# Merging the bursts of a woven recurrence, moving its loads, and giving Pool some subtractions at the start

## The chip, the cores and the metric

The kernel runs on one core of a Trainium2 chip. The metric is the time of one execution on the device in microseconds, the median of three runs. The engines are named as in the profile: PE multiplies matrices, DVE (vector), ACT (scalar) and POOL (GpSimd) do the rest, and SP issues every DMA, all on one queue.

## The reference

One decoder layer for 2048 tokens of width 1024. The normalised input is projected to 4 mLSTM heads (q, k, v, gates o and z) and 2 SSD groups (z, x, B, C, dt, a causal convolution of 4 taps). Each head and each group runs a recurrence over chunks of 128 tokens; both results are gated, normalised, put beside each other, projected back and added to the input.

```python
h = rms_norm(x, norm_w[l])
proj = h @ w_in[l]
...
hm = mlstm_chunkwise(q, k, v, log_i, log_f)            # per head: C <- s_old C + s_loc k^T v; h = (S v + q C) / denom
hm = hm * lax.rsqrt(jnp.mean(hm * hm, axis=-1, keepdims=True) + EPS)
hm = hm * mlstm_norm_w[l] * sigmoid(o_pre) * silu(z_m)
...
y = ssd_chunked(xs, dt, A, Bm, Cm)                     # per group: H <- exp(a) H + B^T (decay x dt); y = (C B^T * decay) x dt + C H
y = (y + d_skip * xs) * silu(z_s)
y = y * lax.rsqrt(mean over the group of y * y + EPS) * ssd_norm_w[l]
x = x + concatenate([hm, y]) @ w_out[l]
return rms_norm(x, final_norm_w)
```

## The kernel before, in words

**The products.** The input projection and the output projection are done as 68 jobs of 7 products each, after Strassen: 2 halves of the tokens (s = 0, 1) with 26 column pairs each (4 pairs for each head h0 to h3, 5 for each group g0, g1, in the phases h0, g0, h1, h2, h3, g1), then 16 jobs of the output projection. A product is 12 matmuls of 128x512 (L270): each operand is split into a high and a low part (names ending in h and l), and high times high, high times low and low times high are summed. The right operands of a product are named R11, R21, R22 and T1 to T4 (token side; they stay in L390 DMA R22h<-ws0R_186 128x2048
L390 DMA R22l<-ws0R_186 128x2048
L346 DMA gd_1_111<-oa 128x1024
L346 DMA gd_1_111<-ob 128x1024
L390 DMA T4h<-ws0T_187 128x2048
L390 DMA T4l<-ws0T_187 128x2048
L788 DMA gin<-gd_1_111 128x6x128
L795 DMA E<-arow_150 128x1024
L803 DMA ea<-arow_150 64x4x128 x2UF for a stage and are loaded anew, "refilled", L390, when the stage changes), the left ones L11, L12, L22 and S1 to S4 (weight side; formed anew for every job: ACT copies the high part, L191, DVE subtracts for the low part, L192). After a product its result pj is taken out by ACT copies (L276, L283, L289, into oa, ob, ca, cbt) and DVE sums.

**The recurrences.** When a phase is done, its recurrence is run by a generator, rec_head or rec_group, while PE works on the jobs of the next phase: `step`, called once for each product, moves a clock on by one tick and calls `wv.to()`, and the class Weave then runs as many pieces of the generator (up to the next `yield`) as keep it in proportion to the phase (28 steps where four jobs follow, 35 where five, 42 in the output projection). What a piece puts on PE stands between two products; it is called a burst here. In `rec_head`, chunk n has: load (hin L676, nmi L678), scores (PE L694, L696; ACT w L690 from nmi; DVE st L698), memory (PE L714, L716, L718: the numerator and the state), then ACT sums squares (sj L731) and copies (mx L732), POOL scales (L733 to L735, mx), gate (loads and forms g, L742), and turn (PE transposes mx, L751; DVE multiplies by the gate, L752; a DMA stores it into mix, L753). In `rec_group`, chunk n has: load (gin L788), decay (DMA E L795, DVE L798, ACT exp L800; ea L803, L805), tokens (PE L813, L814, L817; DVE xw, xdt, cbm), then DVE E times cbm (L829), states (PE L845), update (PE L857), outs (PE L872, with 16 matmuls), then DVE and POOL form the gated squares q (L878 to L883), norm (PE L889; DVE r L891; POOL L892 and dg L894), and spread (PE L901; DVE L902; the store L903). A `later(k, ...)` puts a piece k ticks on: gate 1, turn 4, norm 3 and spread 5 ticks after the burst of their chunk.

**The rest.** The first tokens are normalised, turned and split by `start_h` while the first job already runs. From the phase after h1 on, a background generator does the other half's tokens (`next_h`, s = 0) or scales the output weights (`next_w`, s = 1: loads of wg, we L532, ACT scaling L533, splits L396 and L398, stores L537). The order of PE is that of the program. The instructions of the other engines and the DMAs on SP are put in order by the compiler's scheduler; buffers of a tag come from a ring of fixed size, so that a load waits for the last reader of its ring's slot.

Of the kernel before, what the change touches and what calls it, by code (L numbers as in the profile page):

```python
# [69 lines left out]
def hybrid_layer(ctx, tc, x, norm_w, w_in, b_igate, b_fgate, conv_w, conv_b, dt_bias,  # L70
# [32 lines left out]
    def r2(nm, n=512):  # L103
        return mk([P, n], "r2", 7, nm)

    def r1(nm, n=NV):
        return mk([P, 272], "r1", 6, nm)[:, 0:n]

    def r5(nm, n=P):
        return mk([P, n], "r5", 9, nm)  # L110
# [77 lines left out]
    def split(ops, o, src):  # L188
# [3 lines left out]
        nc.vector.tensor_sub(lo, v, hi.bitcast(F32))  # L192
# [156 lines left out]
    def out_pair(L, R, j, c):  # L349
# [18 lines left out]
        for i, t in enumerate((a, b)):  # L368
# [8 lines left out]
            nc.scalar.activation(mk([P, DM], "r2", 7, "fj", BF16), t, AF.Square, accum_out=sq)  # L377
# [23 lines left out]
    def tok_norm(r0, nwb, t):  # L401
# [3 lines left out]
        jk = mk([P, DM], "r2", 7, "jk", BF16)  # L405
# [17 lines left out]
    def start_h():  # L423
# [14 lines left out]
        def put(o, c, src):  # L438
# [3 lines left out]
            nc.vector.tensor_sub(lo, v, hi.bitcast(F32))  # L442
# [77 lines left out]
    def next_w():  # L520

        for j in range(2):
            for k in range(4):
# [4 lines left out]
                for a in range(2):  # L528
                    r = j * 8 + a * 4 + k
                    for b in range(2):  # L530
                        u = q[a, b]
                        nc.sync.dma_start(u, w_out[r * P:(r + 1) * P, b * TB:(b + 1) * TB])  # L532
                        nc.scalar.activation(u, u, AF.Copy, scale=nwo[:, r:r + 1])  # L533
                yield
# [133 lines left out]
    def rec_head(s, h):  # L668
# [3 lines left out]
        def load(n):  # L672
# [4 lines left out]
            nmi = r2("nmi", 2 * P).rearrange("p (a l) -> p a l", a=2)  # L677
# [29 lines left out]
        def memory(n):  # L707
# [11 lines left out]
            if C is None:  # L719
                C = S["C"] = mk([P, NV + 14], "C", 1, "C")[:, 0:NV]  # L720
# [10 lines left out]
            nc.scalar.activation(mk([P, DV], "r5", 9, "sj", BF16), nps[:, 0:DV], AF.Square, accum_out=sq)  # L731
# [23 lines left out]
        load(0)  # L755
        S["C"] = None
        if s:
            C = S["C"] = mk([P, NV + 14], "C", 1, "C")[:, 0:NV]
            nc.sync.dma_start(C, cd[h])
# [5 lines left out]
        for n in range(len(seq)):  # L765
            if n + 1 < len(seq):
                scores(n + 1)
# [3 lines left out]
            later(1, lambda n=n: gate(n))  # L771
            later(4, lambda n=n: turn(n))
            if n + 3 < len(seq):
                load(n + 3)
            yield

    def rec_group(s, g):
# [128 lines left out]
        decay(0)  # L906
        S["H"] = None
# [7 lines left out]
        for n in range(len(seq)):  # L915
            states(n)
            yield
            update(n)
# [3 lines left out]
            later(3, lambda n=n: norm(n))  # L922
            later(5, lambda n=n: spread(n))
# [6 lines left out]
            yield  # L930

# [3 lines left out]
    NREC = {"h": 10, "g": 25}  # L935

    class Weave:
# [3 lines left out]
        def set(self, g, n, total):  # L941
            self.finish()
            self.g, self.n, self.done, self.i, self.total = g, n, 1, 0, total
# [90 lines left out]
    for n, jb in enumerate(jobs):  # L1034
# [35 lines left out]
        if more:  # L1070
            next(jobs[n + 1]["gen"])
            step(n + 1, "R21")
        next(g)
# [4 lines left out]
        if "s" in jb and (n + 1 == len(jobs) or jobs[n + 1].get("ph") != jb["ph"]):  # L1078
            nxt = [k for k in jobs[n + 1:] if k.get("ph") == jobs[n + 1].get("ph") and k["stage"] == jobs[n + 1]["stage"]]
            wv.set(rec(jb["s"], jb["ph"]), NREC[jb["ph"][0]], 7 * len(nxt) if "s" in jobs[n + 1] else 42)  # L1080
# [35 lines left out]
```

## Time and profile before

| | |
|---|---|
| median of 3 runs | 1832.38 us (1822.41 to 1832.39) |
| profiled execution, its own time | 1829.99 us |
| its span, first to last instruction | 1828.2 us |
| mean granted TensorE clock | 0.966 |
| busy: PE / DVE / ACT / POOL | 1679.5 (92%) / 1308.7 (72%) / 880.6 (48%) / 450.2 us (25%) |
| DMA | 405.32 MB, mean 222 GB/s |

The span leaves out 1.8 us of the execution's own time. PE's busy time is that of its matmuls as the trace shows them; where the granted clock is below 1.00 the same matmul takes longer. Idle time of PE is split in the view of waits by what came last before the matmul that waited.

### The profile page before, as it was taken

The numbers are of one execution on the slowest core, as the hardware profiler recorded it, in microseconds if no ns is written. First come the engines' busy times: TensorE is split into PE (matmuls) and PEld (weight loads), VectorE is DVE, ScalarE is ACT, GpSimd is POOL, SyncE is SP. The second block draws the span as 40 slices with busy tenths as digits, with TensorE's granted clock in tenths as the row PEclk, the third lists the DMA queues.
The fourth block names the chain that finished last, engine by engine and source line by source line (L and its number), as shares of the span: only waits on it lengthen the run. The fifth ranks groups of instructions, "written<-read, shape, count | busy, mean of one in ns | idle before, by whom it ended". The sixth has DMA issues, their size and how long they took to land.

```text
span 1828.2 us, 25057 instructions
## 1 busy us (share of the span) xinstructions
PE 1679.5 (92%) x8072; PEld 1357.2 (74%) x8072; DVE 1308.7 (72%) x2417; ACT 880.6 (48%) x1880; POOL 450.2 (25%) x629
## 2 busy tenths in 40 slices
PE   4999999999899798989899999898988889997997
PEld 4688887778788685767788777777776667776885
DVE  7677968877567693888675895655678578864775
ACT  5344644456566663434564444655565433332443
POOL 2000413332122131223121331202211144532222
PEclk9999999999999899999999999999999989998999
DMA  5245666668787689655575658888877976678543
GB/s 153 93 156 174 185 212 203 207 212 256 224 258 231 181 274 379 206 182 179 161 203 185 196 181 272 290 278 263 258 260 250 384 260 212 205 265 315 189 158 115
DMA packets 358323, 405.32 MB, mean 222 GB/s; under 512 B 30224, under 2 KB 284432, under 8 KB 352816
## 3 DMA queue, kind: packets, MB, share of 16 engines
q1 hardware_dynamic: 358192, 403.72, 68.1%
q8 instruction: 64, 1.05, 0.2%
q14 instruction: 67, 0.55, 0.1%
HBM read 251.40 MB, written 152.24 MB: 221 GB/s over the span
## 4 chain that ended last, share of the span: by engine, by line
PE 25%; DMA 15%; DVE 7%; issue 3%; ACT 2%; SPq 1%; POOL 1%; DVEq 0%; POOLq 0%; ACTq 0%
PE pj L270 21%; DMA E<-arow 1%; DMA we<-in_w_out 1%; DVE E L798 1%; DMA nmi<-mrow 1%; DMA mx<-mix 1%; DMA gin<-gd 1%; DMA ws1R<-hqh 1%; DMA T4l<-ws1T 1%; DMA ws0T<-hql 1%; DMA ws0R<-hqh 1%; DMA ws0T<-hqh 1%; DMA xr<-in_x 1%; DMA ws1T<-hqh 1%; PE rc L872 1%
## 5 line engine op out<-in xcount | busy, mean ns | idle before, releaser
L733 POOL TENSOR_SCALAR sq<-dn,sq 128x1 f32<-128x1 f32 x64 | 46.1, 720 | 624.9 <-ACT sj L731 477.8
L270 PE MATMUL pj<-R22h,S4h 128*128 128x512 f32 x272 | 119.7, 440 | 38.1 <-ACT ob L289 24.6
L270 PE MATMUL pj<-T2h,S2h 128*128 128x512 f32 x272 | 113.4, 417 | 11.6 <-ACT ca L276 9.3
L270 PE MATMUL pj<-T1l,S1h 128*128 128x512 f32 x272 | 107.3, 395 | 7.6 <-DMA T1l<-ws1T 7.2
L270 PE MATMUL pj<-R22l,S4h 128*128 128x512 f32 x272 | 113.1, 416 | 0.0
L270 PE MATMUL pj<-T4h,L22h 128*128 128x512 f32 x272 | 111.5, 410 | 1.4 <-DMA T4h<-ws1T 1.4
L270 PE MATMUL pj<-R11h,L11h 128*128 128x512 f32 x272 | 112.7, 414 | 0.0
L270 PE MATMUL pj<-R22h,S4l 128*128 128x512 f32 x272 | 112.7, 414 | 0.0
L270 PE MATMUL pj<-T2l,S2h 128*128 128x512 f32 x272 | 109.0, 401 | 4.0 <-DMA T2l<-hsT 3.3
L270 PE MATMUL pj<-T1h,S1h 128*128 128x512 f32 x272 | 111.0, 408 | 1.4 <-ACT cbt L283 1.4
L270 PE MATMUL pj<-R21h,L12h 128*128 128x512 f32 x272 | 110.1, 405 | 0.0
L270 PE MATMUL pj<-T3h,S3h 128*128 128x512 f32 x272 | 109.3, 402 | 0.0
L270 PE MATMUL pj<-T2h,S2l 128*128 128x512 f32 x272 | 108.6, 399 | 0.0
L270 PE MATMUL pj<-T1h,S1l 128*128 128x512 f32 x272 | 107.2, 394 | 1.3 <-DVE S1l L192 1.3
L270 PE MATMUL pj<-T4l,L22h 128*128 128x512 f32 x272 | 106.6, 392 | 1.9 <-DMA T4l<-ws1T 1.9
L270 PE MATMUL pj<-T4h,L22l 128*128 128x512 f32 x272 | 106.7, 392 | 0.0
L270 PE MATMUL pj<-R11h,L11l 128*128 128x512 f32 x272 | 106.6, 392 | 0.0
L270 PE MATMUL pj<-R11l,L11h 128*128 128x512 f32 x272 | 106.5, 391 | 0.0
L270 PE MATMUL pj<-T3h,S3l 128*128 128x512 f32 x272 | 106.3, 391 | 0.0
L270 PE MATMUL pj<-R21l,L12h 128*128 128x512 f32 x272 | 106.3, 391 | 0.0
L270 PE MATMUL pj<-R21h,L12l 128*128 128x512 f32 x272 | 106.3, 391 | 0.0
L270 PE MATMUL pj<-T3l,S3h 128*128 128x512 f32 x272 | 106.3, 391 | 0.0
(330 smaller groups left out, 4697.4 us busy)
## 6 DMA issues: line engine op xcount, KB each, us to landing
wa<-in_w_in SPq DMA_DIRECT2D x52, 512.0 KB, 6.2
s<-sum SPq DMA_DIRECT2D x52, 512.0 KB, 5.3
hd<-ob SPq DMA_DIRECT2D x32, 512.0 KB, 3.8
E<-arow SPq DMA_DIRECT2D x32, 512.0 KB, 5.2
hin<-hd SPq DMA_DIRECT2D x64, 256.0 KB, 4.7
mx<-mix SPq DMA_DIRECT2D x32, 512.0 KB, 4.9
wb<-in_w_in SPq DMA_DIRECT2D x26, 512.0 KB, 4.2
sum<-ls SPq DMA_DIRECT2D x26, 512.0 KB, 4.6
```

What stands on the lines that cost most here:

```text
L270: nc.tensor.matmul(ps, lhsT=l[:, k, :], rhs=r[:, k, :], start=start and k + n == 0, stop=k == 3 and n == 2, skip_group_check=True)
L733: nc.gpsimd.tensor_scalar(sq, dn, DV * EPS, sq, op0=ALU.mult, op1=ALU.add)
L798: nc.vector.tensor_scalar(E[:, r, :], E[:, r, :], G["cum"][:, c, k:k + 1], 0.0, op0=ALU.subtract, op1=ALU.min)
L872: nc.tensor.matmul(yps[o:o + HD, (r // 2) * P:(r // 2 + 1) * P], lhsT=xdt[:, r * HD:(r + 1) * HD], rhs=E[:, r, :], start=True, stop=True, ...
```

## The change

In `rec_head` turn(n-1) now stands at the head of the burst with scores(n+1) and memory(n), and gate(n) in the same burst; the deferred calls are gone. In `rec_group` norm(n-1) stands ahead of states(n), and spread(n-1) ahead of update(n) and outs(n). The generators have more pieces (12 and 29), and Weave begins with two of them counted as done. The recurrence of a phase is created, and its first load issued, before the last two products of the phase's last job (`pre`). The scaling of output weights is put three yields behind their loads. Rings change (r2 7 to 6, r1 6 to 8 with nmi moved there, r5 9 to 8, C shares a tag with H). In the first tokens the low parts of T1 to T4 (16 subtractions), and of the left operands as long as the clock stands at 0 (6 subtractions: L11, L12 and S2, S3 of job 0, L11 of job 1, S1 of job 0), go from DVE to POOL. The ring sizes in calls are cut from the diff below.

```diff
@@ -101,13 +101,13 @@
         return mk([P, 1024], "t", 1, nm)
 
     def r2(nm, n=512):
-        return mk([P, n], "r2", 7, nm)
+        return mk([P, n], "r2", 6, nm)
 
     def r1(nm, n=NV):
-        return mk([P, 272], "r1", 6, nm)[:, 0:n]
+        return mk([P, 272], "r1", 8, nm)[:, 0:n]
 
     def r5(nm, n=P):
-        return mk([P, n], "r5", 9, nm)
+        return mk([P, n], "r5", 8, nm)
 
     ident = cst.tile([P, P], F32, name="ident")
     make_identity(nc, ident)
...
@@ -189,7 +189,7 @@
         hi, lo = (mk([P, 4, P], "lr", 10, o + k, F32R) for k in "hl")
         v = src.rearrange("p (k c) -> p k c", k=4)
         nc.scalar.copy(hi, v)
-        nc.vector.tensor_sub(lo, v, hi.bitcast(F32))
+        (nc.vector if clock[0] else nc.gpsimd).tensor_sub(lo, v, hi.bitcast(F32))
         ops[o] = (hi, lo)
 
     def left_sums(ops, a, b, save=None):
...
@@ -439,7 +439,7 @@
             hi, lo = (t[:, :, c * P:(c + 1) * P] for t in R[o])
             v = src.rearrange("p (k c) -> p k c", k=4)
             nc.scalar.copy(hi, v)
-            nc.vector.tensor_sub(lo, v, hi.bitcast(F32))
+            (nc.gpsimd if o[0] == "T" else nc.vector).tensor_sub(lo, v, hi.bitcast(F32))
 
         for c in range(NCH):
             tok_norm(None, nwb, xs[c])
...
@@ -530,8 +530,12 @@
                     for b in range(2):
                         u = q[a, b]
                         nc.sync.dma_start(u, w_out[r * P:(r + 1) * P, b * TB:(b + 1) * TB])
-                        nc.scalar.activation(u, u, AF.Copy, scale=nwo[:, r:r + 1])
-                yield
+                for _ in range(3):
+                    yield
+                for a in range(2):
+                    r = j * 8 + a * 4 + k
+                    for b in range(2):
+                        nc.scalar.activation(q[a, b], q[a, b], AF.Copy, scale=nwo[:, r:r + 1])
 
                 def dst(o, i, v):
                     nc.sync.dma_start(wsd[j][o][:, i, k, :], v)
...
@@ -674,7 +678,7 @@
             o = (b % 2) * TB + c * P
             t = r2("hin").rearrange("p (a l) -> p a l", a=4)
             nc.sync.dma_start(t, hd[s][h][:, 0:4, o:o + P])
-            nmi = r2("nmi", 2 * P).rearrange("p (a l) -> p a l", a=2)
+            nmi = r1("nmi", 2 * P).rearrange("p (a l) -> p a l", a=2)
             nc.sync.dma_start(nmi, mrowd[b][:, h, c * P:(c + 1) * P].partition_broadcast(P))
             L["in", n] = (t, nmi)
 
...
@@ -717,7 +721,7 @@
             cps = rc_tile()
             nc.tensor.matmul(cps[:, 0:NV], lhsT=kw, rhs=vt, start=True, stop=True)
             if C is None:
-                C = S["C"] = mk([P, NV + 14], "C", 1, "C")[:, 0:NV]
+                C = S["C"] = mk([P, GW], "H", 1, "C")[:, 0:NV]
                 nc.vector.tensor_copy(C, cps[:, 0:NV])
             else:
                 nc.vector.scalar_tensor_tensor(C, C, nmi[:, 1, P - 1:P], cps[:, 0:NV],
...
@@ -728,7 +732,7 @@
                                            op0=ALU.mult, op1=ALU.max)
             mx = r1("mx")[:, 0:DV]
             sq = mk([P, 1], "sq", 3, "sq")
-            nc.scalar.activation(mk([P, DV], "r5", 9, "sj", BF16), nps[:, 0:DV], AF.Square, accum_out=sq)
+            nc.scalar.activation(mk([P, DV], "r5", 8, "sj", BF16), nps[:, 0:DV], AF.Square, accum_out=sq)
             nc.scalar.copy(mx, nps[:, 0:DV])
             nc.gpsimd.tensor_scalar(sq, dn, DV * EPS, sq, op0=ALU.mult, op1=ALU.add)
             nc.gpsimd.tensor_tensor(sq, sq, mhalf, op=ALU.pow)
...
@@ -753,9 +757,10 @@
             nc.sync.dma_start(mixd[0][b * NCH + c][:, 2 * h:2 * h + 2, :], g)
 
         load(0)
+        yield
         S["C"] = None
         if s:
-            C = S["C"] = mk([P, NV + 14], "C", 1, "C")[:, 0:NV]
+            C = S["C"] = mk([P, GW], "H", 1, "C")[:, 0:NV]
             nc.sync.dma_start(C, cd[h])
         yield
         scores(0)
...
@@ -763,16 +768,19 @@
         load(2)
         yield
         for n in range(len(seq)):
+            if n:
+                turn(n - 1)
             if n + 1 < len(seq):
                 scores(n + 1)
             memory(n)
             if s == 0 and n + 1 == len(seq):
                 nc.sync.dma_start(cd[h], S["C"])
-            later(1, lambda n=n: gate(n))
-            later(4, lambda n=n: turn(n))
             if n + 3 < len(seq):
                 load(n + 3)
+            gate(n)
             yield
+        turn(len(seq) - 1)
+        yield
 
     def rec_group(s, g):
         seq = [(2 * s + i, c) for i in range(2) for c in range(NCH)]
...
@@ -904,6 +912,7 @@
 
         load(0)
         decay(0)
+        yield
         S["H"] = None
         if s:
             H = S["H"] = mk([P, GW], "H", 1, "H")
...
@@ -913,14 +922,16 @@
         load(1)
         yield
         for n in range(len(seq)):
+            if n:
+                norm(n - 1)
             states(n)
             yield
+            if n:
+                spread(n - 1)
             update(n)
             if s == 0 and n + 1 == len(seq):
                 nc.sync.dma_start(hdd[g], S["H"])
             outs(n)
-            later(3, lambda n=n: norm(n))
-            later(5, lambda n=n: spread(n))
             if n + 1 < len(seq):
                 decay(n + 1)
                 yield
...
@@ -928,11 +939,16 @@
                 if n + 2 < len(seq):
                     load(n + 2)
             yield
+        yield
+        norm(len(seq) - 1)
+        yield
+        spread(len(seq) - 1)
+        yield
 
     def rec(s, ph):
         return rec_head(s, int(ph[1])) if ph[0] == "h" else rec_group(s, int(ph[1]))
 
-    NREC = {"h": 10, "g": 25}
+    NREC = {"h": 12, "g": 29}
 
     class Weave:
         def __init__(self):
...
@@ -940,7 +956,7 @@
 
         def set(self, g, n, total):
             self.finish()
-            self.g, self.n, self.done, self.i, self.total = g, n, 1, 0, total
+            self.g, self.n, self.done, self.i, self.total = g, n, 2, 0, total
             next(g)
 
         def to(self):
...
@@ -1070,17 +1086,21 @@
         if more:
             next(jobs[n + 1]["gen"])
             step(n + 1, "R21")
+        ends = "s" in jb and (not more or jobs[n + 1].get("ph") != jb["ph"])
+        if ends:
+            pre = rec(jb["s"], jb["ph"])
+            next(pre)
         next(g)
         step(n, "R22")
         next(g)
         step(n, "T4")
         next(g, None)
-        if "s" in jb and (n + 1 == len(jobs) or jobs[n + 1].get("ph") != jb["ph"]):
+        if ends:
             nxt = [k for k in jobs[n + 1:] if k.get("ph") == jobs[n + 1].get("ph") and k["stage"] == jobs[n + 1]["stage"]]
-            wv.set(rec(jb["s"], jb["ph"]), NREC[jb["ph"][0]], 7 * len(nxt) if "s" in jobs[n + 1] else 42)
+            wv.set(pre, NREC[jb["ph"][0]], 7 * len(nxt) if "s" in jobs[n + 1] else 42)
             if jb["ph"] == "h1":
                 bgq = next_w() if jb["s"] else next_h()
-                total = 64 if jb["s"] else 84
+                total = 80 if jb["s"] else 84
                 for i in range(total):
                     at(3 + i * 76 // total, bgq)
         if jb["stage"] == 2 and n + 1 < len(jobs) and jobs[n + 1]["stage"] == 3:
```

PE, one chunk of the recurrence of group g0 in the second half (rc is the PSUM tile of a burst, gin and E are as above; the lines left out are products, L270). Before:

```order
L813 MATMUL rc<-gin 128x128
L814 MATMUL rc<-ident,gin 128x128
L817 MATMUL rc<-ident,gin 128x128 x4
...
L901 MATMUL rc<-dg,ones 128x128
L845 MATMUL rc<-gin,H 128x128 x4
...
L889 MATMUL rc<-ones,q 128x1
L857 MATMUL rc<-xw,bt 128x512
L872 MATMUL rc<-E,xdt 64x128 x8
```

The same place after:

```order
L821 MATMUL rc<-gin 128x128
L822 MATMUL rc<-ident,gin 128x128
L825 MATMUL rc<-ident,gin 128x128 x4
...
L897 MATMUL rc<-ones,q 128x1
L853 MATMUL rc<-gin,H 128x128 x4
...
L909 MATMUL rc<-dg,ones 128x128
L865 MATMUL rc<-xw,bt 128x512
L880 MATMUL rc<-E,xdt 64x128 x8
```

The square sums (norm, now L897) have moved ahead of the states (L853), and the spread (now L909) from its own place ahead of the states to a place ahead of the update (L865) and the outputs (L880).

PE, the first two chunks of the recurrence of a head (h0, first half; vt, kw and qp are v, the weighted k and the scaled q; products left out). Before, then after:

```order
L694 MATMUL rc<-hin 128x128
L696 MATMUL rc<-ident,hin 128x128 x3
L714 MATMUL rc<-vt,st 128x258
L718 MATMUL rc<-vt,kw 128x258
...
L694 MATMUL rc<-hin 128x128
L696 MATMUL rc<-ident,hin 128x128 x3
L714 MATMUL rc<-vt,st 128x258
L716 MATMUL rc<-C,qp 128x258
L718 MATMUL rc<-vt,kw 128x258
...
L751 MATMUL rc<-ident,mx 128x128 x2
```

```order
L698 MATMUL rc<-hin 128x128
L700 MATMUL rc<-ident,hin 128x128 x3
L718 MATMUL rc<-vt,st 128x258
L722 MATMUL rc<-vt,kw 128x258
...
L755 MATMUL rc<-ident,mx 128x128 x2
L698 MATMUL rc<-hin 128x128
L700 MATMUL rc<-ident,hin 128x128 x3
L718 MATMUL rc<-vt,st 128x258
L720 MATMUL rc<-C,qp 128x258
L722 MATMUL rc<-vt,kw 128x258
```

Before, the turn (L751) of the first chunk comes after the second chunk's memory (L714 to L718) and a further product; after, the turn (now L755) is the first of the burst that holds the second chunk's memory, two products behind its own.

DVE in the recurrence of g0, first half, before and after (E is the decay, r the norm's sum, y the output of the group):

```order
L829 TENSOR_TENSOR E<-E,cbm 128x1024
L902 TENSOR_TENSOR y<-rc,y 128x512
L847 TENSOR_TENSOR ea<-rc,ea 128x512
L192 TENSOR_TENSOR L11l<-wa,L11h 128x512
L848 TENSOR_TENSOR y<-y,ea 128x512
L891 TENSOR_SCALAR r<-rc 128x1
```

```order
L837 TENSOR_TENSOR E<-E,cbm 128x1024
L192 TENSOR_TENSOR S3l<-wa,S3h 128x512
L899 TENSOR_SCALAR r<-rc 128x1
L855 TENSOR_TENSOR ea<-rc,ea 128x512
L192 TENSOR_TENSOR L11l<-wa,L11h 128x512
L856 TENSOR_TENSOR y<-y,ea 128x512
L910 TENSOR_TENSOR y<-rc,y 128x512
```

Before, the spread's last step (L902) stands behind E times cbm (L829) and ahead of r (L891) of the next chunk; after, r (L899) follows E times cbm (L837) and a subtraction for a left operand, and the spread's last step (L910), which needs that r, comes last.

SP, at the change from the last phase to the output projection, before and after:

```order
L390 DMA R22h<-ws0R_186 128x2048
L390 DMA R22l<-ws0R_186 128x2048
L346 DMA gd_1_111<-oa 128x1024
L346 DMA gd_1_111<-ob 128x1024
L390 DMA T4h<-ws0T_187 128x2048
L390 DMA T4l<-ws0T_187 128x2048
L788 DMA gin<-gd_1_111 128x6x128
L795 DMA E<-arow_150 128x1024
L803 DMA ea<-arow_150 64x4x128 x2
```

```order
L757 DMA mix_15_127<-g 128x256
L796 DMA gin<-gd_1_111 128x6x128
L803 DMA E<-arow_150 128x1024
L390 DMA R22h<-ws0R_186 128x2048
L390 DMA R22l<-ws0R_186 128x2048
L346 DMA gd_1_111<-oa 128x1024
L346 DMA gd_1_111<-ob 128x1024
L390 DMA T4h<-ws0T_187 128x2048
L390 DMA T4l<-ws0T_187 128x2048
```

The loads of gin and E for the first chunk stood behind the refills of R22 and T4; they stand ahead of them now.

## Rows read from the trace of the kernel before

**Rows 1.** The page, part 1: busy time of each engine, share of the span, instructions.

```profile
PE 1679.5 (92%) x8072; PEld 1357.2 (74%) x8072; DVE 1308.7 (72%) x2417; ACT 880.6 (48%) x1880; POOL 450.2 (25%) x629
```

**Rows 2.** Busy time by stretch: PE, PEld, DVE, ACT, POOL, PEclk, DMA share, GB/s.

```profile
20.00:40.00 20.00, 11.04 (x56) 9.15 (x56) 19.11 (x35) 11.23 (x22) 3.27 (x5) 0.91 0.49 86
1260.00:1280.00 20.00, 14.88 (x63) 11.96 (x62) 9.18 (x24) 9.27 (x22) 5.84 (x10) 0.89 0.80 256
```

**Rows 3.** Waits of PE: total us, times, longest us.

```profile
PE pj L270 <- ACT ob L289: 24.6, 10, 5.9
PE pj L270 <- ACT cbt L289: 13.4, 5, 5.4
PE rc L813 <- DMA gin<-gd: 12.0, 1, 12.0
PE rc L901 <- POOL dg L894: 4.1, 4, 1.7
PE rc L872 <- DVE E L829: 3.4, 4, 1.3
PE rc L751 <- POOL mx L735: 2.0, 1, 2.0
```

**Rows 4.** Waits of all engines, same columns.

```profile
ACT w L690 <- DMA nmi<-mrow: 91.7, 36, 5.5
ACT we L533 <- DMA we<-in_w_out: 11.4, 7, 5.8
```

**Rows 5.** Timeline, 1262 to 1280 us: start, us, instruction, idle before it and releaser.

```profile
1266.36 0.30 ACT L690 ACTIVATE w<-nmi,u 128x1 f32<-128x1 f32 x1 [4.04 <-DMA nmi<-mrow]
1276.39 0.79 PE L270 MATMUL pj<-R22h,S4h 128*128 128x512 f32 x1 [5.12 <-ACT ob L289]
```

**Rows 6.** Chain that ended last, 1240 to 1250 us: start, us, what.

```profile
1242.48 0.43 PE rc L718 x2
1242.91 5.47 PE pj L270 x24
1248.38 0.22 PE rc L751 x2
```

**Rows 7.** Instructions of three lines of a head: duration min/median/max, first and last start.

```profile
L718 PE MATMUL rc<-vt,kw x128: 381/381/485, 175.6 to 1432.1; 128*128 128x258 f32 x128
L735 POOL TENSOR_SCALAR mx<-mx,sq x64: 932/1040/4320, 182.0 to 1440.4; 128x256 f32<-128x256 f32 x64
L751 PE MATMUL rc<-ident,mx x128: 270/272/421, 188.9 to 1443.6; 128*128 128x128 f32 x128
```

**Rows 8.** Timeline, one chunk of a group, 1011 to 1026 us.

```profile
1011.77 0.28 PE L889 MATMUL rc<-ones,q 128*128 128x1 f32 x2
1012.99 1.09 PE L872 MATMUL rc<-E,xdt 128*64 128x128 f32 x16
1014.12 0.34 SPq L795 DMA_DIRECT2D E<-arow  x1
1014.73 0.61 POOL L894 TENSOR_SCALAR dg<-ident,r 128x128 f32<-128x128 f32 x1
1022.96 1.22 DVE L829 TENSOR_TENSOR E<-E,cbm 128x1024 f32<-128x1024 f32 x1
1025.41 1.09 PE L872 MATMUL rc<-E,xdt 128*64 128x128 f32 x16
```

**Rows 9.** Timeline, change to the output projection, 1452 to 1468 us.

```profile
1452.62 0.71 SPq L788 DMA_DIRECT2D gin<-gd  x1
1467.55 0.79 PE L813 MATMUL rc<-gin 128*128 128x128 f32 x2 [12.01 <-DMA gin<-gd]
```

**Rows 10.** Timeline of DVE and POOL, 55 to 56 and 1710 to 1712 us.

```profile
55.45 0.69 DVE L442 TENSOR_TENSOR T1l<-t,T1h 128x512 fp32r<-128x512 f32 x1
...
1710.55 1.54 POOL L372 TENSOR_TENSOR oa<-oa,xr 128x512 f32<-128x512 f32 x1 [1.55 <-DVE oa L380]
1710.84 1.80 DVE L192 TENSOR_TENSOR L12l<-mx,L12h 128x512 fp32r<-128x512 f32 x1
```

More of the change, by code (lines that the diff above doesn't have):

```diff
@@ L376, in out_pair @@
             sq = mk([P, 1], "fsq", 2, "fsq")
-            nc.scalar.activation(mk([P, DM], "r2", 7, "fj", BF16), t, AF.Square, accum_out=sq)
+            nc.scalar.activation(mk([P, DM], "r2", 6, "fj", BF16), t, AF.Square, accum_out=sq)
             nc.gpsimd.tensor_scalar(sq, sq, 1.0 / DM, EPS, op0=ALU.mult, op1=ALU.add)
@@ L404, in tok_norm @@
         ss = mk([P, 1], "ss", 4, "ss")
-        jk = mk([P, DM], "r2", 7, "jk", BF16)
+        jk = mk([P, DM], "r2", 6, "jk", BF16)
         nc.scalar.activation(jk, t, AF.Square, accum_out=ss)
```

## The prediction, made blind

> **What bounds the kernel now.** I read the page's busy times first: PE is busy 1679.5 of 1828.2 us, 92%, and no other engine more than 72% [rows 1]. So PE is the bound, and only two things can move the time: what PE waits for, and the clock that it is granted behind such waits. The view of PE's waits comes next. The reader is to see there that the two largest groups, 24.6 us in 10 waits and 13.4 us in 5, are products that wait for ACT to take a result out (L289), that one wait for gin takes 12.0 us, and that the recurrences' own chains hardly reach PE: 4.1 us for dg, 3.4 us for E times cbm, 2.0 us for a turn's mx [rows 3]. The view of all waits says what ACT itself stood for: 91.7 us in 36 waits for nmi (L690) and 11.4 us for output weights (L533) [rows 4]. One such stretch is seen in the timeline: ACT sits 4.04 us until nmi lands at 1266.36, and PE sits 5.12 us until 1276.39 for an ACT copy [rows 5]. In the 20 us around it PE is busy 14.88 us at a clock of 0.89 [rows 2]. A loss on PE therefore costs more than its idle time there: 20 x (1 - 0.89) = 2.2 us more for each such wait.
>
> **The change, part by part.** All sums are against the profiled execution, 1829.99 us, which lies 2.4 us under the median; I add them to the median in the end.
>
> *Fewer bursts.* A turn of a head takes 0.22 us on PE by itself [rows 6], and the same matmuls run in the merged burst. What goes is at most the start of a burst; I take -1.5 us for 64 turns and 32 chunks of norm and spread, an estimate, with 0 and -3 as ends (0.02 to 0.03 us each, no row shows more).
>
> *The turn of a head.* Before, mx has a long time: from the first memory matmul of the first chunk (175.6 us) to the start of its mx on POOL (182.0) it is 6.4 us, to its turn (188.9) 13.3 us; for the last chunk 8.3 and 11.5 us [rows 7]. From memory's end to mx's end the 64 chunks have a median of 6.95 us; the first and the last are those of the rows, with some 0.5 us of memory taken off and 1 us of POOL added. After the change the turn stands behind its memory by two products, in the recurrences that run beside five jobs partly by three. Two products are 5.47 us [rows 6]. The median chunk is then 6.95 - 5.47 = 1.5 us late, and 64 x 1.5 = 95 us is the most that this gives in that way. It won't be reached: half the recurrences have five jobs, where some gaps are three products, 8.2 us; and while PE stands, ACT and DVE work off what stands ahead of the chain, so that the next chunk is earlier. I take a third, +30 us. Ends: +10 (mx late only in the densest stretches, before has one such wait of 2.0 us [rows 3]) and +60.
>
> *nmi and the output weights.* nmi now has slots of its own in r1, and the scaling has three yields between load and use. Of PE's 24.6 + 13.4 = 38 us for L289 [rows 3], 15 waits, I count the whole as hung on ACT's two waits at most, and with 2.2 us of clock for some seven of them, some -53. But the load of nmi still stands on SP between stores of weights and of mix, and ACT's w is still ahead of the copies in part of the chunks; half goes, -27 us. Ends: 0, where nmi lands no earlier, and -45.
>
> *The recurrence of a group.* In the chunk shown, outs end at 1012.99 + 1.09 = 1014.08, the next E is loaded from 1014.12 on, and E times cbm ends at 1022.96 + 1.22 = 1024.18: a chain of 10.1 us. The next outs start at 1025.41, 11.3 us after the last [rows 8], three products of 2.73 us (half of 5.47 [rows 6]) and some bursts. Weave's numbers now spread the eight outs of a recurrence over 18 steps in place of 21 where four jobs follow: three of seven gaps lose a product and have 11.3 - 2.73 = 8.6 us for the chain of 10.1. Each is 1.5 us late; and norm to dg, 1012.05 to 1015.34 = 3.3 us [rows 8], now lies ahead of update and outs, with one product and the states between (2.73 us and the states, some 3.6 us by an estimate), or only the states where both bursts fall into one step (two such in a recurrence, 2.4 us late each). r also stands behind E times cbm on DVE in 8 of 21 chunks, which makes one late where the other is. 3 x 1.5 is 4.5, the shared steps add up to 3 where they aren't the same wait: +7.5 for each of three recurrences, +22. The fourth runs beside the output projection with four steps for a gap, where dg alone is tight: +7. Together +29 us. Ends: +5, if loads of E that are issued as before land earlier and DVE is quicker while PE stands, and +60, if chains are as long as in the denser chunks (a wait of 3 to 4 us at seven gaps of three recurrences).
>
> *Loads ahead of the phase's last two products.* gin's load was issued at 1452.62 behind the refills, and PE waited 12.0 us until 1467.55 [rows 9]. Issued ahead of them, it costs about a third of that. But those refills then start behind gin and E, and the products R22 and T4 of the next stage need them: of the 8 us that are won I leave 6, -6 us, with -12 and +3 as ends (+3 where at the other stage change a refill that was in time is late).
>
> *The first tokens.* DVE is busy 19.11 of 20 us there, PE 11.04 and POOL 3.27 [rows 2]. 22 subtractions of 0.6 us in a row (0.69 alone [rows 10]) leave DVE, 13 us; on POOL a subtraction of two such tiles takes 1.54 us in the row shown, so four a chunk are 6 us, within the 10 us that a chunk takes. PE waits for them still, since T1 and T2 are used at once in the last chunk. A collision is to be seen too: while POOL adds two tiles at 1710.55, DVE's subtraction starts at 1710.84 and takes 1.80 us, 1.1 more than alone [rows 10]. I take -2 us, with -5 and +11 as ends (22 x 1.1 = 24 lost less 13 won).
>
> The Trainium skill, "SBUF — State Buffer", section "SBUF: two separate sides", says that a DVE operation with two SBUF inputs and a GpSimd operation share a port pair under an exclusive lock, where the second one blocks wholly. The 1.80 us agree with it; by the rule each of the 22 may block a DVE operation, and the first tokens would come to the upper end above instead of -2.
>
> *Sum.* -1.5 + 30 - 27 + 29 - 6 - 2 = +22.5 us. 1832.4 + 22.5 = 1855 us.
>
> **Rivals.** *The waits of ACT go and nothing takes their place (faster).* The chains have slack that the trace of before doesn't show, because nobody asked for it: turn's 10 to 13 us were given, not needed, and the scheduler puts mx and E earlier when their readers come earlier. Then turn costs +10, the groups +5, ACT's waits give -40, the rest -9.5: -34.5, 1798 us. For it: 38 us stand behind ACT's copies alone [rows 3]. Against it: in the stretches where the gain would be, ACT's order still puts w ahead of copies.
>
> *They cancel (no change).* Half the turn's cost (+15), half the groups' (+15), ACT -25, the rest -7: -2, 1830 us. For it: PE's waits only change their name; against it: the two new chains come in all 96 chunks, the old waits in 15 places.
>
> *The group chain binds in every chunk (slower, more).* If the outs wait for the spread at each of 32 chunks, 2 to 3 us with the clock that goes with them, the groups alone give +60 and the sum +54, 1886 us. It decides from a chain of norm, r and dg of over 6 us, where the room is 3.6; the one shown takes 3.3 [rows 8].
>
> *The merge does nothing by itself and the start is worse:* POOL's chain in the first tokens takes the upper end, +11; the sum is then +35.5, 1868 us.
>
> **How the numbers follow.** Forecast (1855) and the cases above it 0.42, of which the forecast 0.27, the binding group chain 0.10, the start 0.05; cancelling 0.26; faster 0.32. A change within 1%, 18 us, is about what a measurement of this kernel can't tell from none. Predicted is the likeliest side's own case, 1855 (its own range 1842 to 1875). The range: down to 1797, the faster rival with a little more, since 1 in 10 lies below; up to 1888, the binding group chain, with less than 1 in 10 above. Both signs hold much, so it is wide.
>
> **What would show each step right or wrong.** In the profile after: waits of PE for mx (L755 in the new numbers) of some 20 to 30 us in all, for E times cbm, dg or y at the outs and spread (L880, L909) of 20 us and more; waits of ACT for nmi under half of 91.7; those of PE for L289's copies under 20; no wait of over 8 us for gin; DVE below 17 of 20 us in the stretch from 20 to 40 us. The forecast is wrong if PE waits under 10 us for mx and under 15 us for group chains: then the gain on ACT decides, and the time lies under 1825. It is wrong the other way if products themselves wait for DVE's sums.

## The result: 8.2% slower, and the profile after

The changed kernel takes 1979.57 us in the median of four runs (1976.66 to 1985.01), the kernel before 1832.39 us beside it: a ratio of 1.0821, interval 1.0777 to 1.0865. That is 147 us, where +22.5 us were forecast, and it lies above the range. The profiled execution took 1976.66 us, its span is 1974.9 us.

The page of the changed kernel, part 1, answers to [rows 1]:

```profile
PE 1724.8 (87%) x8072; PEld 1381.8 (70%) x8072; DVE 1304.7 (66%) x2395; ACT 881.7 (45%) x1880; POOL 505.2 (26%) x651
```

The matmuls are as many as before, and yet PE is busy 1724.8 - 1679.5 = 45 us longer, at a mean granted clock of 0.945 where it was 0.966. The gaps between its matmuls, summed over the trace, went from 130 to 231 us. So of the 147 us some 101 are waits, and 45 are matmuls that take longer. The clock makes most of these 45: in the records of the granted clock, PE's busy time at the lower of its two levels (1.2 GHz in place of 2.4) went from 86 to 159 us, and half of these 73 us more, some 37, is what the lower level cost. The other 8 us are not settled.

The waits of PE in the changed kernel answer to [rows 3] (total us, times, longest us):

```profile
PE rc L755 <- POOL mx L739: 66.7, 33, 8.3
PE rc L909 <- POOL dg L902: 55.8, 19, 8.0
PE rc L897 <- POOL q L891: 24.8, 8, 6.6
...
PE pj L270 <- ACT cbt L289: 6.9, 3, 3.8
PE pj L270 <- ACT ob L289: 6.0, 5, 1.9
...
PE pj L270 <- DMA R22h<-ws0R: 3.8, 1, 3.8
```

The turn waits 66.7 us for mx (2.0 before), the spread 55.8 us for dg (4.1), the norm 24.8 us for q. The waits for copies (L289) went from 38.0 to 12.9 us, and gin's 12.0 us are gone; in their stead a refill, R22h, is waited for (the right operands of the products stay in SBUF for a stage, and are loaded anew, refilled, when the stage changes). E times cbm is hardly waited for, 1.1 us. ACT's own waits answer to [rows 4]:

```profile
ACT w L694 <- DMA nmi<-mrow: 124.7, 42, 5.6
```

They rose from 91.7 us, where I had them fall below half. The three lines of a head answer to [rows 7] (duration min/median/max, first and last start):

```profile
L722 PE MATMUL rc<-vt,kw x128: 381/381/639, 187.0 to 1558.8; 128*128 128x258 f32 x128
...
L739 POOL TENSOR_SCALAR mx<-mx,sq x64: 929/1120/2868, 192.7 to 1561.6; 128x256 f32<-128x256 f32 x64
...
L755 PE MATMUL rc<-ident,mx x128: 270/273/477, 193.7 to 1567.4; 128*128 128x128 f32 x128
```

In the first chunk mx starts 5.7 us after memory and the turn 6.7 us after it, right behind mx; before it was 6.4 and 13.3. Over all chunks, from the records of both traces, the chains shortened little or not at all, and the room given to them shrank (medians, us; the room ends where PE's next burst starts, so that after the change it holds PE's own wait as well):

| | chain before | after | room before | after |
|---|---|---|---|---|
| memory's end to mx's end / to the turn (64) | 6.95 | 6.32 | 12.9 | 7.1 |
| outs' end to q's end / to the norm (32) | 6.7 | 5.3 | 10.2 | 6.9 |
| norm's end to dg's end / to the spread (32) | 5.2 | 5.4 | 8.3 | 5.7 |
| outs' end to the next E times cbm (28) | 11.9 | 11.0 | | |

The longest wait for dg is seen in the timeline of the changed kernel (start, us, instruction, idle before it and releaser):

```profile
373.25 0.28 PE L897 MATMUL rc<-ones,q 128*128 128x1 f32 x2
373.39 1.14 PE L853 MATMUL rc<-gin,H 128*128 128x128 f32 x8
...
378.32 1.21 DVE L837 TENSOR_TENSOR E<-E,cbm 128x1024 f32<-128x1024 f32 x1
...
380.05 0.15 DVE L899 TENSOR_SCALAR r<-rc 128x1 f32<-128x1 f32 x1
...
380.94 1.53 POOL L902 TENSOR_SCALAR dg<-ident,r 128x128 f32<-128x128 f32 x1
382.53 0.80 PE L909 MATMUL rc<-dg,ones 128*128 128x128 f32 x2 [8.00 <-POOL dg L902]
```

Norm, states and spread stand in one step, with no product between. PE's norm is done at 373.5, but DVE comes to r only at 380.05, behind E times cbm and what that stood behind in DVE's order, and dg is done at 382.5. In the 20 us from 374, which hold this wait, PE is busy 12.00 us and its mean granted clock is 0.74 (stretch, then PE, PEld, DVE, ACT, POOL, PEclk, DMA share, GB/s):

```profile
20.00:40.00 20.00, 12.97 (x60) 10.55 (x58) 15.77 (x23) 11.44 (x23) 11.73 (x12) 0.98 0.55 108
374.00:394.00 20.00, 12.00 (x61) 8.94 (x60) 16.36 (x32) 3.14 (x7) 6.36 (x6) 0.74 0.43 144
```

The first of these two lines answers to the start in [rows 2]: DVE fell from 19.11 to 15.77 us there, POOL rose from 3.27 to 11.73.

Both programs run the same 476 products in the same order, so the starts of equal products can be laid beside each other. The growth of each phase, in us, by the recurrence that runs beside it:

| phase of the products (its recurrence) | first half | second half |
|---|---|---|
| up to job 2 (the first tokens) | 5.9 | |
| h0 (g1 of the first half in the second) | | 31.0 |
| g0 (h0) | 5.0 | -1.3 |
| h1 (g0) | 28.5 | 30.4 |
| h2 (h1) | -0.4 | -0.2 |
| h3 (h2) | 1.3 | 1.9 |
| g1 (h3) | 21.9 | 8.1 |
| output, first 42 products (g1), and the next 14 | | 18.1, -4.5 |

The four stretches beside a group (28.5, 31.0, 30.4, and 18.1 less 4.5) make 104 of the 147 us. I had +29 for them.

### The profile page after: what moved, and what is told of

The parts are those of the page before. It is cut to its first block, busy times and chain, and to the rows that moved or that the text cites. A ratio compares the mean times of both kernels' runs of the same rounds, so it can differ in the third digit from the quotient of the medians.

```text
span 1974.9 us, 25161 instructions
## 1 busy us (share of the span) xinstructions
PE 1724.8 (87%) x8072; PEld 1381.8 (70%) x8072; DVE 1304.7 (66%) x2395; ACT 881.7 (45%) x1880; POOL 505.2 (26%) x651
## 5 line engine op out<-in xcount | busy, mean ns | idle before, releaser
L737 POOL TENSOR_SCALAR sq<-dn,sq 128x1 f32<-128x1 f32 x64 | 56.6, 885 | 678.8 <-ACT mx L736 299.7
L270 PE MATMUL pj<-R22h,S4h 128*128 128x512 f32 x272 | 114.0, 419 | 16.8 <-ACT cbt L289 6.9
L270 PE MATMUL pj<-T2h,S2h 128*128 128x512 f32 x272 | 113.2, 416 | 6.4 <-ACT T2h L441 3.9
L270 PE MATMUL pj<-T1l,S1h 128*128 128x512 f32 x272 | 108.0, 397 | 7.1 <-DMA T1l<-ws1T 7.1
L270 PE MATMUL pj<-T4h,L22h 128*128 128x512 f32 x272 | 111.3, 409 | 2.2 <-DMA T4h<-ws1T 2.2
L270 PE MATMUL pj<-T1h,S1h 128*128 128x512 f32 x272 | 112.9, 415 | 0.0
L270 PE MATMUL pj<-R11h,L11h 128*128 128x512 f32 x272 | 112.0, 412 | 0.0
L270 PE MATMUL pj<-T3h,S3h 128*128 128x512 f32 x272 | 111.1, 408 | 0.0
L270 PE MATMUL pj<-T2l,S2h 128*128 128x512 f32 x272 | 108.5, 399 | 2.9 <-POOL T2l L442 2.9
L270 PE MATMUL pj<-R22l,S4h 128*128 128x512 f32 x272 | 109.4, 402 | 1.7 <-DMA R22l<-ws0R 1.6
L270 PE MATMUL pj<-T4l,L22h 128*128 128x512 f32 x272 | 107.8, 396 | 2.7 <-DMA T4l<-ws1T 1.9
L270 PE MATMUL pj<-R21h,L12h 128*128 128x512 f32 x272 | 109.3, 402 | 0.0
L270 PE MATMUL pj<-R22h,S4l 128*128 128x512 f32 x272 | 109.1, 401 | 0.0
L270 PE MATMUL pj<-R11h,L11l 128*128 128x512 f32 x272 | 108.2, 398 | 0.0
L270 PE MATMUL pj<-T2h,S2l 128*128 128x512 f32 x272 | 108.2, 398 | 0.0
L270 PE MATMUL pj<-R11l,L11h 128*128 128x512 f32 x272 | 108.1, 397 | 0.0
L270 PE MATMUL pj<-T4h,L22l 128*128 128x512 f32 x272 | 107.5, 395 | 0.0
L270 PE MATMUL pj<-T1h,S1l 128*128 128x512 f32 x272 | 107.2, 394 | 0.0
L270 PE MATMUL pj<-T3l,S3h 128*128 128x512 f32 x272 | 106.6, 392 | 0.0
L270 PE MATMUL pj<-T3h,S3l 128*128 128x512 f32 x272 | 106.4, 391 | 0.0
L270 PE MATMUL pj<-R21h,L12l 128*128 128x512 f32 x272 | 106.2, 390 | 0.0
L270 PE MATMUL pj<-R21l,L12h 128*128 128x512 f32 x272 | 106.2, 390 | 0.0
```

Source lines behind the costliest of these rows:

```text
L270: nc.tensor.matmul(ps, lhsT=l[:, k, :], rhs=r[:, k, :], start=start and k + n == 0, stop=k == 3 and n == 2, skip_group_check=True)
L737: nc.gpsimd.tensor_scalar(sq, dn, DV * EPS, sq, op0=ALU.mult, op1=ALU.add)
```

## The experiments

Ratios are to the kernel before on the same chip, each with its 95% interval. The first theory, R: turn, norm and spread have too little room behind the work that feeds them, and that is the loss. The rival, D: denser recurrences, rings and moved loads make the other engines late, and the places of turn, norm and spread only show it.

**Taking the merge out of the changed kernel.** a1_group_apart defers norm and spread again, a2_turn_apart turn and gate, a3_both_apart all.

```diff
# a1
-            if n:
-                norm(n - 1)
             states(n)
...
             outs(n)
+            later(3, lambda n=n: norm(n))
+            later(5, lambda n=n: spread(n))
# a2
-            if n:
-                turn(n - 1)
...
-            gate(n)
+            later(1, lambda n=n: gate(n))
+            later(4, lambda n=n: turn(n))
```

a1_group_apart: 

> The changed kernel, but norm and spread of a group again 3 and 5 ticks after the outs (all else of the change stays). Theory R (too little room: the chains outs to q, norm to dg keep their length, 5 to 7 us, and the places given to norm and spread lie too close behind): the 108 us that the four stretches with a group recurrence lost come back, time 1865 to 1890 us, PE's waits for dg and q under 10 us together. Rival D (denser recurrence, smaller rings or moved loads make the other engines late): the stretches stay long, 1950 to 1985 us.

a2_turn_apart: 

> The changed kernel, but turn of a head again 4 ticks and gate 1 tick after the burst. Theory R: PE's waits for mx (66.7 us) go and with them some 25 us of clock, the copies that PE waits for stay at 13 us: 1885 to 1920 us. Rival D: the head stretches keep their length, 1960 to 1985 us.

a3_both_apart: 

> The changed kernel with all of turn, gate, norm and spread deferred as before: what is left of the change is the denser recurrence, the earlier first load, the rings, the yields ahead of the weight scaling and POOL's subtractions. Theory R: 1790 to 1830 us, the same as before or up to 2% faster (the waits for L289 and gin gone, plus 6 us at the start). Rival D: over 1900 us.

Measured: 1944.21 us, 1.0600 [1.0567, 1.0633]; 1948.14 us, 1.0639 [1.0609, 1.0668]; 1917.12 us, 1.0470 [1.0440, 1.0501]. The places of norm and spread are worth 2.2%, those of turn and gate 1.8%, both together 3.5%. In a1 and a2 the times lie between the two theories, and in a3 D's case came, over 1900 us. R is right on the waits (dg from 55.8 to 5.3 us in a1, mx from 66.7 to 5.0 us in a2), but 4.7% stay when they are gone. In a2 the waits for L289's copies, which I expected to stay at 13 us, are back at 41.9 us: part of the wait for mx only takes their place. In a3 other waits of the group have grown, E times cbm to 22.2 us and xdt to 12.2 us, and those for L289's copies are at 38.9 us. So R alone falls, and what D names has to be taken apart.

**The start.** a4_dve_start puts all subtractions back on DVE in the changed kernel, e2_pool_start moves only them in the kernel before.

```diff
-            (nc.gpsimd if o[0] == "T" else nc.vector).tensor_sub(lo, v, hi.bitcast(F32))
+            nc.vector.tensor_sub(lo, v, hi.bitcast(F32))
```

a4_dve_start: 

> The changed kernel with all low parts formed by DVE as before. If POOL's chain in the first tokens is what shifts the second job by 5.9 us: 5 to 7 us faster than the changed kernel, 1970 to 1975 us. If the shift is of the order of DMAs there or POOL's relief is worth something later: within 2 us of it.

e2_pool_start: 

> The kernel before with the 22 subtractions of the first tokens on POOL, nothing else. If the 5.9 us by which the second job starts later in the changed kernel are POOL's: 3 to 6 us slower, job 2 later by as much, PE waiting for T2l from POOL. If they come of the other edits: within 1 us.

Measured: 1974.03 us, 1.0777 [1.0729, 1.0826], and 1835.86 us, 1.0042 [1.0022, 1.0062]. The time of a4 as a whole can't be told from the changed kernel's, but the starts of its products can: in a4 those of the second job come as before (within 0.2 us, in place of 5.9 late), in e2 they come 5.6 us late. The loss is POOL's: the subtractions alone bring it, and PE waits 2.9 us for T2l from POOL in e2 as in the changed kernel:

```profile
PE pj L270 <- POOL T2l L442: 2.9, 1, 2.9
```

**Each part alone, on the kernel before.** b1_merge_only has the merged bursts, b2_dense_only Weave's pieces, b3_rings_yields the rings and the yields of the weight scaling, b4_early_load the early first load.

```diff
# b2
-    NREC = {"h": 10, "g": 25}
+    NREC = {"h": 12, "g": 29}
-            self.g, self.n, self.done, self.i, self.total = g, n, 1, 0, total
+            self.g, self.n, self.done, self.i, self.total = g, n, 2, 0, total
             next(g)
+            next(g)
# b4
+        if ends:
+            pre = rec(jb["s"], jb["ph"])
+            next(pre)
         next(g)
         step(n, "R22")
```

b1_merge_only: 

> The kernel before with the merged bursts alone (turn with the next chunk's memory, gate at once, norm ahead of states, spread ahead of update and outs; numbers of Weave, rings, loads and the start as before). If merging costs what taking it out of the changed kernel gave back (1979 less 1917): 50 to 70 us, about 1880 to 1905 us. If it costs only in the denser recurrence of the changed kernel: under 20 us, below 1850 us.

b2_dense_only: 

> The kernel before with the changed kernel's Weave alone (12 and 29 pieces, two counted as done, so that the eight outs of a group lie over 18 steps in place of 21; turn, norm and spread deferred as before). If the denser recurrence is what is left of the loss: +40 to +65 us, 1870 to 1900 us, mostly in the four stretches with a group, as waits for E and for xw and xdt. If rings or loads are: under +10 us.

b3_rings_yields: 

> The kernel before with the changed rings (r2 6, r1 8 with nmi, r5 8, C with H) and the yields ahead of the weight scaling alone. If the rings stall loads: +15 to +40 us, 1847 to 1872 us, in the stretch from the first half's g1 phase too, which the other edits left 19 us longer. If the load of nmi gains from its own slots: 10 to 25 us faster, 1807 to 1822 us.

b4_early_load: 

> The kernel before with the first load of each recurrence issued ahead of the phase's last two products, pieces and spacing exactly as before. If the load gains as I forecast: 6 us faster, 1820 to 1830 us, the 12 us wait for gin gone. If refills behind it are late: 0 to +5 us.

Measured: 1882.06 us, 1.0298 [1.0267, 1.0329]; 1859.41 us, 1.0166 [1.0138, 1.0194]; 1866.19 us, 1.0208 [1.0180, 1.0236]; 1833.19 us, 1.0021 [0.9999, 1.0043]. Merging costs at the old spacing too, in waits for dg and mx:

```profile
PE rc L904 <- POOL dg L897: 42.7, 18, 4.8
PE rc L751 <- POOL mx L735: 34.7, 17, 5.9
```

By phases it is +35 us beside groups and +22 us beside heads. Density costs 29 us, less than the 40 that I expected at least; by phases, in one trace, it is +40 us beside groups, and 13 us come back beside heads. Its waits are those for the chunk's operands:

```profile
PE rc L859 <- DVE xdt L826: 15.2, 5, 3.6
PE rc L874 <- DVE E L831: 12.5, 10, 3.1
```

The early load is worth nothing to the whole, as far as the interval tells: the wait for gin goes, and a refill, R22h, is waited for 4.2 us instead, which is what I had as the end of +3.

**Which ring.** c1_r2_ring has r2 6, r1 8 with nmi in it; c2_r5_and_c r5 8 and C in H's tag; c3_weight_yields the three yields alone. d1_r2_8 raises r2 to 8 (with c2's two edits for room), d2_after_r2_7 is the changed kernel with r2 at 7, e1_nmi_r1 moves nmi into r1 with r2 left at 7 (again with c2's edits).

```diff
# c1, and e1 without its first line
-        return mk([P, n], "r2", 7, nm)
+        return mk([P, n], "r2", 6, nm)
-        return mk([P, 272], "r1", 6, nm)[:, 0:n]
+        return mk([P, 272], "r1", 8, nm)[:, 0:n]
-            nmi = r2("nmi", 2 * P)
+            nmi = r1("nmi", 2 * P)
```

c1_r2_ring: 

> The kernel before with ring r2 cut from 7 to 6, r1 raised from 6 to 8 and nmi moved from r2 to r1, nothing else. A chunk of a group takes five tiles of r2 (ea, xw, xdt, y, z). If that ring is the loss of the rings' run (36 us): +20 to +36 us, 1850 to 1867 us, mostly in the stretches beside a group, with more of ACT's waiting for ea and nmi. If the other two parts are: within 5 us of before.

c2_r5_and_c: 

> The kernel before with ring r5 cut from 9 to 8 and C in H's tag, nothing else. If r5 (E, qp, st, kw of a head; bt, cbm, q, dg of a group) or the shared tag is the loss: +10 to +30 us. If r2 is: within 5 us of before, 1826 to 1836 us.

c3_weight_yields: 

> The kernel before with three yields between the loads of output weights and their scaling, nothing else. As I forecast: ACT's wait for wg and we (18 us) gone and up to 10 us faster, 1818 to 1828 us, in the second half's h2 to g1 stretches. If ACT's waits there are those for nmi, whatever the weights do: within 4 us of before.

d1_r2_8: 

> The kernel before with ring r2 raised from 7 to 8; the room comes from r5 9 to 8 and C in H's tag, which cost 0.4% alone. If the ring sets the pace of loads on both sides of 7: as much as 10 to 20 us faster than before, 1805 to 1822 us. If 7 is enough and only 6 is too few: that 0.4%, 1830 to 1840 us.

d2_after_r2_7: 

> The changed kernel with ring r2 back at 7 (nmi stays in r1), nothing else. If the ring costs in the changed kernel what it cost alone (33 us): 1940 to 1955 us. If its cost hides in the waits for turn, norm and spread there, or was that of nmi's other ring: within 10 us of 1979.

e1_nmi_r1: 

> The kernel before with nmi moved from r2 to r1 (r1 6 to 8), r2 left at 7, and r5 8 and C in H's tag to make room (0.4% alone). If nmi's own slots do what I forecast: 10 us or more faster. If sharing r1 with vt, mx and g is what made ACT wait longer for nmi in the changed kernel (91.7 to 124.7 us): +10 to +25 us, 1.0 to 1.8%, and ACT's waits for nmi over 110 us. If neither: about 0.4%.

Measured: c1 1.0179 [1.0131, 1.0226]; c2 1.0037 [1.0016, 1.0058]; c3 1.0011 [0.9990, 1.0032]; d1 0.9959 [0.9935, 0.9984]; d2 1.0629 [1.0574, 1.0684], 1951.65 us; e1 1.0104 [1.0064, 1.0143]. Less c2's 0.4%, nmi in r1 costs some 0.7% (the two intervals leave 0.2 to 1.1%), and ACT's waits for nmi rise from 91.7 us to

```profile
ACT w L690 <- DMA nmi<-mrow: 133.5, 47, 5.3
```

in e1, the opposite of its intent. nmi's load is issued a median 18.0 us ahead of its chunk's scores there, where it was 19.4: slots of its own did not bring it earlier. A larger r2 did shorten these waits, with nmi left in it, in d1:

```profile
ACT w L690 <- DMA nmi<-mrow: 68.2, 31, 4.0
```

The r2 ring from 7 to 6 makes the rest of c1's 1.8%, some 1.1% (0.5 to 1.8%), and 1.9 points in the changed kernel (1.0821 to 1.0629), as waits of loads on SP for their slot's last reader. By phases c1 is +21 us beside groups, where e1, with r2 left at 7, is +3. In the changed kernel, SP's waits for a slot to load z (L885) and ea (L811), which share r2 with xw, read by the update L865, and ACT's for ea; then the same with r2 at 7:

```profile
SPq L811 <- PE rc L865: 24.4, 5, 6.6
...
SPq L885 <- PE rc L865: 17.5, 4, 5.7
```

```profile
ACT ea L813 <- DMA ea<-arow: 73.7, 22, 8.6
```

```profile
SPq L811 <- PE rc L865: 13.6, 3, 4.9
...
SPq L885 <- PE rc L865: 1.9, 1, 1.9
```

```profile
ACT ea L813 <- DMA ea<-arow: 35.5, 17, 5.7
```

The kernel with a ring of 8 is the only one faster than the kernel before, by 0.4% (1831.47 us beside 1839.54), less than 1% and between the two cases that I had. The yields ahead of the scaling do nothing that the interval shows.

**Dose, and what is left.** c4_turn_3ticks moves the turn one tick nearer; d4_sparser starts the recurrences two steps earlier; d3_rest is the changed kernel with merge, density and r2 undone.

```diff
# c4
-            later(4, lambda n=n: turn(n))
+            later(3, lambda n=n: turn(n))
# d4, in both places
-            i = max(0, self.i - 3)
+            i = max(0, self.i - 1)
```

c4_turn_3ticks: 

> The kernel before with turn 3 ticks after its burst in place of 4, nothing merged: some 8.2 us of products behind memory in place of 11, against 5.5 to 8.2 where turns are merged. If only the room counts: the memory to mx times (median 6.95 us, a quarter of them over 10) put some 10 to 15 chunks behind it by 1 to 4 us, +4 to +20 us, 1835 to 1851 us, as waits for mx. If merging as such costs (order on the other engines): within 3 us of before.

d4_sparser: 

> The kernel before with Weave's offset of 3 steps cut to 1, so that a group's eight outs lie over 23 steps in place of 21 beside four jobs, nothing else. If room between outs is what the kernel lacks even before: 5 to 15 us faster, 1812 to 1825 us. If before has room enough, or the earlier first pieces wait for their loads: within 5 us, or slower by the wait.

d3_rest: 

> The changed kernel with turn, gate, norm and spread deferred, Weave's numbers and ring r2 as before: what is left is the early first load, POOL's subtractions at the start, the yields ahead of the weight scaling, r5, C's tag and nmi in r1. If merging (52 us), density (30) and r2 (33) are the loss: 1830 to 1850 us. If a loss stays that only the whole shows: over 1860 us.

Measured: 1.0063 [1.0038, 1.0088]; 1.0115 [1.0070, 1.0161]; 1.0171 [1.0126, 1.0216]. One tick less costs 0.6%, by waits for mx that rise from 2.0 us to

```profile
PE rc L751 <- POOL mx L735: 29.6, 16, 5.1
```

while those for L289's copies fall from 38.0 to 25.3: the room counts without any merging, and a part of a wait only changes its name. Sparser isn't better by itself. Some 9 us of its 1.1% are that the first piece of a recurrence comes sooner behind its load, and PE waits for gin 20.7 us in place of 12.0; the waits for mx rise too, from 2.0 to 9.6 us, and the rest is open, so that this run doesn't tell what more room between outs is worth:

```profile
PE rc L813 <- DMA gin<-gd: 20.7, 2, 19.8
```

d3 came out above the range for merging, density and r2 as the whole loss; its 1.7% is what e1 (1.0), e2 (0.4), b4 (0.2) and c3 (0.1) make together, so that these parts lose nothing together that they don't lose alone.

## Why the prediction was wrong

**The sum.** By the parts made alone the change is 1.0298 x 1.0166 x 1.0208 x 1.0021 x 1.0042 = 1.075, against 1.082 measured; the rest, 0.6%, is about what the intervals leave open. R and D are both needed: merging is 3.0%, density 1.7, rings 2.1. Beside groups these three alone make 35 + 40 + 25 = 100 of the 104 us. Two steps of the prediction failed. The term of -27 us took it that nmi in r1 would free PE of its waits for copies; the rings and yields cost some 38 us instead. The term of +29 us took the group's chains to be only a little longer than their room; merge and density cost some 75 to 80 us there.

*Fewer bursts* (-1.5): no run shows this term by itself. In the chunk shown there was none to have for norm and spread: the order of PE before has them already in one burst with update and outs, and with the states.

*The turn* (+30): the mechanism is the forecast one, and the net cost meets the term: taking it out of the changed kernel gives 1.8%, some 33 us, and the head stretches of b1 grew by 22 us. The lateness was read off a distribution of 64 chains, not off one. But the third that I took of it was chosen, not worked out, and the wait was 66.7 us where I had 20 to 30; that the net is so near is in part luck, since the waits for copies shrank beside it.

*nmi and the output weights* (-27): this step failed in its reason. nmi's own slots don't bring it earlier, and ACT waits longer for it (+0.7%); the yields are worth +0.1%. I had counted the whole 38 us of the copies' waits as hung on ACT's waits for nmi and the weights. In the trace of before, ACT stood for nmi in the 10 us ahead of only six of these 15 waits, 17.3 us of the 38, and for we alone ahead of one more, 4.4 us. Nor do the two go together in the runs: in d1 the waits for nmi fell to 68.2 us and those for copies rose to 45.5. The copies' waits of PE did fall from 38.0 to 12.9 us in the changed kernel, but while PE stood elsewhere: in e1 (41.3 us) and c3 (37.4 us), without the merge, that gain isn't there, and in b1, with the merge and without nmi's move, most of it is (19.2 us). The cost of rings cut elsewhere to make room, r2 above all, was not in the sum at all: I counted what nmi gains and not what ea, xw, xdt, y, z and hin lose. With it the step is +38 us in place of -27. How r1's other tiles hold nmi back I did not settle.

*The group* (+29): right in sign, mis-sized nearly three times. Norm and spread are worth 2.2% in the changed kernel, some 40 us (35 beside groups in b1), and density another 40 us beside groups in b2. Two readings failed. I took norm to dg from one chunk, 3.3 us, where the median of 32 is 5.2, so that I saw room where none was; the third rival was to decide by a chain of over 6 us, and 10 of the 32 chains before lie above that. That rival comes nearest to what happened: PE waits for dg at 19 of 32 chunks. And the norm's wait for q (median 6.7 us before, with a room of two products) had no term, though it came to 24.8 us. The clock that goes with waits I priced at ACT's stalls, not here.

*The early load* (-6): the wait for gin went as forecast, a refill took its place: +0.2%.

*The first tokens* (-2): +0.4%, 6 to 8 us, nearer to the upper end of +11. DVE was relieved, 15.77 us, but POOL's subtractions became what PE waits for. Their price I took from a row of 1.54 us that is an addition (L372), and one beside a DVE operation; alone a subtraction takes 1.27 us. The collision that the upper end priced is there (lines of the changed kernel, duration min/median/max):

```profile
L410 DVE SCALAR_TENSOR_TENSOR xt<-xt,ss,nwb x4: 1284/2288/2309, 21.6 to 49.9; 128x1024 f32<-128x1024 f32 x4
```

```profile
L442 POOL TENSOR_TENSOR T3l<-t,T3h x4: 1278/2262/2280, 30.7 to 62.2; 128x512 fp32r<-128x512 f32 x4
```

The normalisation xt takes 2.29 us in the median where four of four took 1.28 before, and POOL's T3l 2.26 where its neighbour T2l takes 1.27. The Trainium skill, "SBUF — State Buffer", section "SBUF: two separate sides", has an exclusive lock on the shared port pair, with the second one blocked. Both rows agree with it: each engine loses about 1 us to the other. In the last chunk DVE then stands 2.37 us until T2l has read the tile t, which DVE's next sum (L465) writes: what DVE was relieved of, it waits for.

*Cancelling* was the rival that the L289 waits speak for: they fell as others rose, but were outweighed. Its sum had -7 for the rest where the terms give -9.5; that decides nothing.

## What to carry to other kernels

A piece that is merged into a neighbour's burst saves at most its own start, which no run here shows, and pays with the room behind the work that feeds it: compare that room with the distribution of the chain, its upper quarter, not with one example. A buffer ring that is cut to feed another one is a term of the sum: count the tiles in flight in each loop that uses it. Parts that each look like a gain should be run alone, on the old kernel: four of the five cost here, and none gained.

## What the runs showed that I had not expected

Waits cost more than themselves: 101 us more of gaps went with 45 us more of matmul time at 0.945 in place of 0.966, with a dip to 0.74 in the 20 us that hold one 8 us wait. The price isn't fixed: in b1 41 us more of gaps went with 16 us, in c4 12 us with none. And a chain doesn't shorten much when PE stands: memory to mx went only from 6.95 to 6.32 us, although PE waited for it 33 times; outs to q fell more, from 6.7 to 5.3 us.
